# Moving the adaptive norm's sums to GpSimd beside mixer and queries and to VectorE beside the gated stage, with row sums behind their chunk's split

## Chip, cores and metric

One core of a Trainium2 chip runs the whole kernel. The metric is device time in microseconds of one execution. Engines carry the profile's names: PE (TensorE), DVE (VectorE), ACT (ScalarE), POOL (GpSimd) and SP (SyncE, which issues most loads).

## What is computed

Two blocks on 512 tokens of width 1024, in float32. The first block has a mixer (convolution and pooling), a feed-forward layer that picks 16 of 16384 experts for each of 8 heads and token, and a gated projection. The second has two attention layers, each with an adaptive norm whose shift, scale and gate come from a condition vector for the tokens and one for a context of 256 rows. Cut to what matters:

```python
h = h + concat([y_conv, y_pool]) @ w_o                     # mixer
# experts, on xn = rms_norm(h)
q = (xb @ w_q).reshape(T, 8, 2, 128)                       # queries
s = einsum('thpd,hpkd->thpk', q, sub_keys)                 # scores; top 16, pairs, top 16 again
act = gelu(einsum('thkd,td->thk', expert_u[eidx], xb))
h = h + einsum('thk,thkd->td', gate * act, expert_v[eidx])
# gated stage
h = h + sigmoid(rms_norm(h) @ w_ple_gate) * (p @ w_ple_proj)
# second block, for layer i in (0, 1); the same for the context rows with c_ctx
shift, scale, gate = split(silu(c) @ ada_w[i] + ada_b[i], 3)
hx = rms_norm(x, norm_g[i]) * (1 + scale) + shift
x = x + gate * attention_i(hx, hc)
```

`ada_w` is 2 x 1024 x 3072. The change concerns how `silu(c) @ ada_w` is summed, and when.

## The kernel before

The stages follow one another: mixer, queries, expert chunks, expert products, gated stage, attention A, attention B. Matrix products in float32 are made of two halves: ACT writes the rounded high half (`wh`, line 93), DVE subtracts it for the low one (`wl`, line 94), and three matmuls are summed (lines 104 to 106). Each engine works through its instructions in order; a planner sets that order when the program is built, from the order of the code, from due times and from `issue_after`, which puts an instruction behind another on its engine.

**Mixer** (`mix`). The 16 column blocks of `w_in` go through `proj`, then `w_o` by token blocks of 128. When a token block is complete, `norm.add` begins the next normalisation: ACT sums squares, POOL takes the row scale in two small instructions (`rstat`, lines 112 and 113, written `rn`), DVE scales (`xs`), and PE flips the result into `x`. POOL's other work here is two casts, eight fills and these row scales.

**Queries and chunks** (`peer`). Sixteen queries, each with one chunk of `expert_u` beside it; then the routing of four token blocks with the rest of the 128 chunks (`chunk`). Tokens 0 to 127 are done by rows that are gathered (class `Gathered`): for each of 128 choices a row per token of `expert_r` comes by a gather on POOL and DVE takes a dot product (line 442); later a row of `expert_v` comes and DVE adds it, weighted, into `h` (line 453, `sums`). Tokens 128 to 511 (384 columns) go through all 16384 experts: gate weights are written out to `Gd` and activations to `Hd`, both in DRAM. A pace factor of 1.2 sets how many gathers go beside one unit of routing.

**Products** (`peer_out`). For each of the 128 chunks a load brings `gt` (every fourth chunk) and `ht` (every second) from `Gd` and `Hd`, DVE multiplies them (`pr`, line 702), the product is split (`xn_0h`, `xn_0l` to `xn_7l`), `expert_v` is loaded and split (`wl`), and 18 matmuls follow (lines 715, 716, 718). Row sums are drawn at 1.1 a chunk. Here, too, the adaptive norm's sums lie: 48 loads of 512 KB (`araw`, on SP's queue), 88 scalings or multiply-adds on DVE (`aacc`, lines 777 and 780; one operand column per 128 rows of `ada_w`), then folds of partition halves through ACT copies and POOL additions (lines 796 to 802). One step is drawn for every pair of chunks.

**Gated stage** (`ple`) and after. Between its token blocks `finish` turns the sums into columns by small matmuls, adds the biases and keeps shift and scale in `ada_aff` and the gate in DRAM. Attention A begins with its weights (`a_qkv`) on the same SP queue, and its last step is `gate_residual`.

## Time and profile before

| | us |
|---|---|
| median of 3 runs (lowest, highest) | 2477.11 (2474.19, 2484.84) |
| the profiled execution, its own time | 2475.35 |
| its span, first to last instruction | 2473.6 |
| PE busy in it | 2264.6 |
| DVE busy in it | 1897.8 |
| POOL busy in it | 739.8 |

The span is what the trace shows; the execution's time has 1.8 us around it. Busy times are sums over a span in which several stages with different limits follow one another; a stage is read by its own stretch of the trace. The mean granted TensorE clock is 0.968 of full speed.

### The profile page before, as it was taken

How to read it: one execution, taken by the hardware profiler on the slowest of the kernel's cores; microseconds unless marked ns; L12 is line 12 of the kernel's file. 1: busy time of each engine (PE TensorE's matmuls, PEld its weight loads, DVE VectorE, ACT ScalarE, POOL GpSimd, SP SyncE). 2: the span in 40 equal slices, each digit the busy share in tenths (PEclk: the TensorE clock that was granted, in tenths of full speed). 3: DMA queues.
4: the chain of work that ended last, by engine and by line, in shares of the span. 5: the costliest groups of instructions: out<-in, count | busy, mean ns of one | idle time of the engine just before them, and what ended most of it. 6: DMA issues, size and time to landing. Idle time of an engine off the chain costs nothing. (4 is left out here: it accounts for less than half of the span.)

```text
span 2473.6 us, 34866 instructions
## 1 busy us (share of the span) xinstructions
PE 2264.6 (92%) x12611; PEld 1972.5 (80%) x12611; DVE 1897.8 (77%) x3431; ACT 1082.1 (44%) x1876; POOL 739.8 (30%) x745
## 2 busy tenths in 40 slices
PE   8999997999998939878888789989999999999997
PEld 6888887999998938766777567777888788898886
DVE  5567799999998879897988885473488955378884
ACT  4243333444443423332333333452477834466772
POOL 1000005334334452352443540031233323023331
PEclk9999998999999979999999899999999999999999
DMA  4233338999999899979989785332211032210002
GB/s 161 94 102 120 115 133 292 340 376 345 342 362 346 326 374 332 326 257 331 321 319 341 267 307 187 103 105 96 92 33 31 24 104 89 82 48 27 26 10 94
DMA packets 179084, 481.08 MB, mean 194 GB/s; under 512 B 15437, under 2 KB 68957, under 8 KB 177376
## 3 DMA queue, kind: packets, MB, share of 16 engines
q1 hardware_dynamic: 125840, 276.95, 32.9%
q0 software_dynamic: 42128, 151.57, 16.7%
q10 hardware_dynamic: 10944, 50.34, 5.0%
q8 instruction: 99, 1.62, 0.3%
q14 instruction: 73, 0.60, 0.1%
HBM read 419.02 MB, written 59.78 MB: 194 GB/s over the span
## 5 line engine op out<-in xcount | busy, mean ns | idle before, releaser
L93 ACT ACTIVATE wh<-raw 128x1024 fp32r<-128x1024 f32 (+2 forms) x371 | 388.6, 1050 | 705.1 <-DMA raw<-in_expert_v 180.8
L94 DVE TENSOR_TENSOR wl<-raw,wh 128x1024 fp32r<-128x1024 f32 (+2 forms) x371 | 453.4, 1226 | 124.2 <-ACT wh L93 119.8
L429 POOL DMA_INDIRECT grow<-in_expert_v,gidx x128 | 214.0, 1672 | 357.7 <-DVE h L453 312.1
L429 POOL DMA_INDIRECT grow<-in_expert_r,gidx x128 | 168.1, 1313 | 254.0 <-DVE gdot L442 229.9
L453 DVE SCALAR_TENSOR_TENSOR h<-grow,gdot,h 128x1024 f32<-128x1024 f32 x128 | 172.4, 1347 | 30.7 <-DMA grow<-in_expert_v,gidx 30.1
L442 DVE CUSTOM_DVE_ANT_0 gjunk<-grow,gx 128x1024 bf16<-128x1024 f32 x128 | 156.3, 1221 | 14.8 <-DMA grow<-in_expert_r,gidx 14.6
L929 DVE TENSOR_TENSOR ptl<-acc,pth 128x512 fp32r<-128x512 f32 x184 | 123.7, 687 | 30.5 <-ACT pth L928 29.0
L780 DVE SCALAR_TENSOR_TENSOR aacc<-araw,silu_c,aacc 128x1024 f32<-128x1024 f32 x77 | 97.7, 1282 | 54.1 <-DMA araw<-in_ada_w 53.9
L928 ACT ACTIVATE pth<-acc 128x512 fp32r<-128x512 f32 x184 | 106.3, 596 | 51.1 <-PE acc L1457 31.4
L1094 POOL TENSOR_SCALAR p<-p,st 128x256 f32<-128x256 f32 (+2 forms) x96 | 65.0, 678 | 135.8 <-DVE st L1093 96.3
L1438 POOL TENSOR_SCALAR p<-p,st 128x768 f32<-128x768 f32 x64 | 60.5, 946 | 127.0 <-DVE st L1437 104.1
L644 ACT ACTIVATE hs<-acc 128x384 f32<-128x384 f32 x128 | 61.1, 478 | 76.7 <-PE acc L106 76.5
L702 DVE TENSOR_TENSOR pr<-ht,gt 128x384 f32<-128x384 f32 x128 | 81.2, 653 | 2.3 <-DMA ht<-Hd 1.9
L106 PE MATMUL acc<-xn_0h,wl 128*128 128x384 f32 (+2 forms) x175 | 61.3, 350 | 23.5 <-DVE wl L94 23.5
L1092 ACT ACTIVATE p<-S,st 128x257 f32<-128x257 f32 (+2 forms) x96 | 62.9, 655 | 25.3 <-DVE st L1090 14.3
L524 POOL CAST sif<-si 128x256 bf16<-128x256 uint32 x4 | 6.5, 1633 | 200.8 <-DVE si L520 173.7
L613 PE MATMUL g<-oh,oh 128*128 128x128 f16 x768 | 54.6, 222 | 13.0 <-DVE oh L606 8.2
L104 PE MATMUL acc<-xn_0h,wh 128*128 128x384 f32 (+2 forms) x175 | 64.3, 367 | 1.3 <-ACT hs L644 1.1
L112 POOL TENSOR_SCALAR rn<-rn 128x1 f32<-128x1 f32 x34 | 10.8, 318 | 182.0 <-ACT xs L111 176.3
L1434 DVE TENSOR_REDUCE st<-S 128x1 f32<-128x768 f32 x64 | 60.8, 951 | 5.3 <-PE S L106 4.2
L1090 DVE TENSOR_REDUCE st<-S 128x1 f32<-128x257 f32 (+2 forms) x96 | 61.6, 643 | 3.5
L613 PEld LDWEIGHTS <-oh 128*128 128x128 f16 x768 | 46.0, 99 | 21.5 <-issue 12.6
(1144 smaller groups left out, 7606.9 us busy)
## 6 DMA issues: line engine op xcount, KB each, us to landing
raw<-in_expert_u SPq DMA_DIRECT2D x128, 512.0 KB
raw<-in_expert_v SPq DMA_DIRECT2D x128, 512.0 KB
Hd<-hs ACTq DMA_DIRECT2D x64, 384.0 KB
Gd<-gs ACTq DMA_DIRECT2D x12, 2048.0 KB
gt<-Gd SPq DMA_DIRECT2D x32, 768.0 KB
ht<-Hd SPq DMA_DIRECT2D x64, 384.0 KB
araw<-in_ada_w SPq DMA_DIRECT2D x48, 512.0 KB
raw<-in_w_in SPq DMA_DIRECT2D x16, 512.0 KB
```

Of the source, the lines that this page charges most:

```text
L93: nc.scalar.activation(hi[:, s], src[:, s], AF.Copy)
L94: (sub or nc.vector).tensor_tensor(lo[:, s], src[:, s], hi[:, s].bitcast(F32), OP.subtract)
L104: mm(out, a[0], b[0], start=start, stop=False)
L429: self.k.nc.gpsimd.indirect_dma_start(t, None, table, at)
L442: nc.vector.tensor_tensor_reduce(junk, t, self.x, 1.0, 0.0, OP.mult, OP.add, self.dot[:, s : s + 1])
L453: nc.vector.scalar_tensor_tensor(self.h, t, self.dot[:, s : s + 1], self.h, OP.mult, OP.add)
L613: nc.tensor.matmul(g[:, i], oh[2][at], oh[q][at], start=q == 0, stop=q == 1)
L702: nc.vector.tensor_tensor(by_g(pr), by_g(cur["h"][:, c % 2]), cur["g"][:, :, c % GC], OP.mult)
L780: nc.vector.scalar_tensor_tensor(a, raw, sc, a, OP.mult, OP.add)
L928: k.nc.scalar.activation(hi, src, AF.Copy)
L929: (eng or k.nc.vector).tensor_tensor(lo, src, hi.bitcast(F32), OP.subtract)
L1094: nc.gpsimd.tensor_scalar(p[:, :W], p[:, :W], st[:, 2:3], 1.0, OP.mult, OP.mult)
```

## The change

The sums of the adaptive norm leave `peer_out`. They are made on halves of 128x512 now. Layer 0 and the gate third of layer 1 are summed by POOL alone (a scaling and an addition for each term, loads on POOL's own queue), drawn two steps at a time in the mixer's projections, between token blocks of `w_o` and behind each query. Shift and scale of layer 1 are summed by DVE (multiply-adds of 128x512, loads on SP's queue) between token blocks of the gated stage and of the start of attention A. Sums go to DRAM; `finish(layer)` loads them back in halves of 64 rows, adds the halves on DVE and goes on by small matmuls, for layer 0 in the gated stage and for layer 1 in the last step of attention A. Besides, each row sum stands behind the low half of the newest split, the pace factor goes from 1.2 to 1.5, and in the mixer the buffer `c` is single and the product `yc` is made in place. The diff, cut to its core (the removed bodies of `work`, `fold` and `finish` are described above):

```diff
@@ split
-            (sub or nc.vector).tensor_tensor(lo[:, s], src[:, s], hi[:, s].bitcast(F32), OP.subtract)
+            self.wl = (sub or nc.vector).tensor_tensor(lo[:, s], src[:, s], hi[:, s].bitcast(F32), OP.subtract).ins
@@ rstat
-        nc.gpsimd.tensor_tensor(out, out, self.mhalf[:, :1], OP.pow)
+        self.rs = nc.gpsimd.tensor_tensor(out, out, self.mhalf[:, :1], OP.pow).ins
@@ mix
+        def some(n):
+            for _ in range(n):
+                next(work, None)
+
         def proj(nb):
             uh, ul = unit if nb == 12 else k.unit(ap["w_in"][nb])
+            some(2)
             return now(k.fm(x, 8, uh, ul, [0]))
...
-            c = mp.tile([P, T], F32, tag="c", name=k.nm("c"), bufs=2)
+            c = mp.tile([P, T], F32, tag="c", name=k.nm("c"), bufs=1)
...
-            yc = mp.tile([P, T], F32, tag="yc", name=k.nm("yc"), bufs=2)
-            nc.vector.tensor_tensor(yc, y, psb, OP.mult)
-            put_split(k, *yf.run(g, 0), yc)
+            nc.vector.tensor_tensor(y, y, psb, OP.mult)
+            put_split(k, *yf.run(g, 0), y)
...
-        k.tm(yf, 8, [tm_units(ap["w_o"], 4 * nh, 2, 4) for nh in range(2)], range(TB), evac)
+        units = [tm_units(ap["w_o"], 4 * nh, 2, 4) for nh in range(2)]
+        k.tm(yf, 8, units, range(TB), evac, between=8 * [lambda: some(2)])
@@ Gathered.sums
-            nc.vector.scalar_tensor_tensor(self.h, t, self.dot[:, s : s + 1], self.h, OP.mult, OP.add)
+            with self.k.tc.issue_after(self.k.wl):
+                nc.vector.scalar_tensor_tensor(self.h, t, self.dot[:, s : s + 1], self.h, OP.mult, OP.add)
@@ peer
-                    spent -= c * 1.2
+                    spent -= c * 1.5
...
         query(hp)
+        for _ in range(2):
+            next(work, None)
         chunk(c)
         c += 1
+    for _ in work:
+        pass
...
-    adp = adx.enter_context(tc.tile_pool(name="adp", bufs=1, side="right"))
-    ada = Ada(k, adp, hs[1])
@@ peer_out
-            if c < NCH - 2:
-                next(ada, None)
-        for _ in ada:
-            pass
@@ Ada
-    def work(self, pool):
+    def work(self, pool, thirds, gpsimd):
...
+        for layer, third, half in [(l, t, s) for l, t in thirds for s in range(2)]:
+            conds = self.conds(layer, third)
+            at = third * 1024 + half * 512
+            acc = [pool.tile([P, 512], F32, tag="aacc", name=k.nm("aacc"), bufs=2) for _ in conds]
+            for kc in range(8):
+                raw = pool.tile([P, 512], F32, tag="araw", name=k.nm("araw"), bufs=3)
+                w = k.ap["ada_w"][layer, kc, :, at : at + 512]
+                if gpsimd:
+                    with k.tc.issue_after(k.rs):
+                        nc.gpsimd.dma_start(raw, w)
+                else:
+                    nc.sync.dma_start(raw, w)
+                for cond, a in enumerate(acc):
+                    sc = self.s[:, cond * 8 + kc : cond * 8 + kc + 1]
+                    if kc == 0:
+                        (nc.gpsimd if gpsimd else nc.vector).tensor_scalar(a, raw, sc, 1.0, OP.mult, OP.mult)
+                    elif gpsimd:
+                        t = raw
+                        if cond + 1 < len(conds):
+                            t = pool.tile([P, 512], F32, tag="atmp", name=k.nm("atmp"), bufs=1)
+                        nc.gpsimd.tensor_scalar(t, raw, sc, 1.0, OP.mult, OP.mult)
+                        nc.gpsimd.tensor_tensor(a, a, t, OP.add)
+                    else:
+                        nc.vector.scalar_tensor_tensor(a, raw, sc, a, OP.mult, OP.add)
                 yield
-                if third == 1:
-                    self.fold(pool, self.acc[layer, 0, 0], pair[0], 32)
-                    yield
-        self.fold(pool, self.acc[0, 0, 2], pair[0], 32)
+            for cond, a in enumerate(acc):
+                nc.gpsimd.dma_start(self.parts[layer, third, half][cond], a)
+            yield
-    def finish(self):
+    def finish(self, layer):
...
+            def folded(third, half):
+                t = [fp.tile([P, 512], F32, tag="afold", name=k.nm("afold"), bufs=4) for _ in range(2)]
+                m = 64 * len(self.conds(layer, third))
+                for i in range(2):
+                    for c in range(m // 64):
+                        s = slice(64 * c, 64 * c + 64)
+                        nc.sync.dma_start(t[i][s], self.parts[layer, third, half][c, 64 * i : 64 * i + 64])
+                nc.vector.tensor_tensor(t[0][:m], t[0][:m], t[1][:m], OP.add)
+                return t[0][:m], sel[:m, third]
@@ ple
-            ada.finish()
-            adx.close()
+            ada.finish(0)
+            apool = adx.enter_context(tc.tile_pool(name="adq", bufs=1, side="right"))
+            rest.append(ada.work(apool, [(1, 0), (1, 1)], False))
...
+        def later():
+            for _ in range(2):
+                next(rest[0], None)
...
-        k.tm(x, 8, units, range(TB), evac, between=[before.pop(0), conditions, context])
+        k.tm(x, 8, units, range(TB), evac, between=[before.pop(0), conditions, context] + 5 * [later])
...
-    return [lambda: flip(0), lambda: flip(1), norm[0].close]
+    return [lambda: flip(0), lambda: flip(1), norm[0].close] + 13 * [later] + [end]
@@ gate_residual
+                    if tb == 5:
+                        ada.finish(1)
@@ the whole kernel
+        ada = Ada(k)
+        work = ada.work(adx.enter_context(tc.tile_pool(name="adp", bufs=1, side="right")), [(0, 0), (0, 1), (0, 2), (1, 2)], True)
         qw = Query(k)
-        before, xs = mix(k, h, x, qw.load)
-        ada, before, pT = peer(k, h, x, adx, qw, before, xs)
+        before, xs = mix(k, h, x, qw.load, work)
+        before, pT = peer(k, h, x, work, adx, qw, before, xs)
```

On POOL, around the row scale of the first token block that comes out of the mixer (`rn_1068` before, `rn_1338` after; `u` and `z` are the mixer's tiles, `araw` a load of `ada_w`, `atmp` a scaled term, `aacc` a sum). Before:

```order
L305 MEMSET u_710 128x8
L306 MEMSET u_710 128x8
L342 MEMSET z_827 128x1
L343 MEMSET z_827 128x1
L112 TENSOR_SCALAR rn_1068<-rn_1068 128x1
L113 TENSOR_TENSOR rn_1068<-rn_1068,mhalf 128x1
L112 TENSOR_SCALAR rn_1100<-rn_1100 128x1
L113 TENSOR_TENSOR rn_1100<-rn_1100,mhalf 128x1
```

After:

```order
L795 TENSOR_TENSOR aacc_1236<-aacc_1236,araw_1241 128x512
L795 TENSOR_TENSOR aacc_1235<-aacc_1235,atmp_1276 128x512
L794 TENSOR_SCALAR araw_1274<-araw_1274,silu_c 128x512
L794 TENSOR_SCALAR atmp_1283<-araw_1281,silu_c 128x512
L795 TENSOR_TENSOR aacc_1236<-aacc_1236,araw_1274 128x512
L795 TENSOR_TENSOR aacc_1235<-aacc_1235,atmp_1283 128x512
L794 TENSOR_SCALAR araw_1281<-araw_1281,silu_c 128x512
L795 TENSOR_TENSOR aacc_1236<-aacc_1236,araw_1281 128x512
L112 TENSOR_SCALAR rn_1338<-rn_1338 128x1
L113 TENSOR_TENSOR rn_1338<-rn_1338,mhalf 128x1
```

Before, the row scale follows the last fill. After it, 72 scalings, 62 additions and 44 issues of loads and stores of the adaptive norm stand between the first norm and it, and between it and the last of the four row scales another ten, eight and seven.

On DVE, in the middle of the products (`h_58` is the sum of token block 0, `pr` the product of gate and activation). Before:

```order
L777 TENSOR_SCALAR aacc_10437<-araw_10435,silu_c 128x1024
L94 TENSOR_TENSOR wl_10380<-raw_10377,wh_10379 128x1024
L777 TENSOR_SCALAR aacc_10439<-araw_10435,silu_c 128x1024
L929 TENSOR_TENSOR xn_2l_95<-pr_10516,xn_2h_94 128x384
L453 SCALAR_TENSOR_TENSOR h_58<-grow_11014,gdot,h_58 128x1024
L929 TENSOR_TENSOR xn_3l_97<-pr_10547,xn_3h_96 128x384
L94 TENSOR_TENSOR wl_10411<-raw_10408,wh_10410 128x1024
L702 TENSOR_TENSOR pr_10617<-ht_10584,gt_10582 128x384
L702 TENSOR_TENSOR pr_10654<-ht_10652,gt_10582 128x384
L453 SCALAR_TENSOR_TENSOR h_58<-grow_11045,gdot,h_58 128x1024
L780 SCALAR_TENSOR_TENSOR aacc_10437<-araw_10510,silu_c,aacc_10437 128x1024
```

After:

```order
L94 TENSOR_TENSOR wl_11039<-raw_11036,wh_11038 128x1024
L460 SCALAR_TENSOR_TENSOR h_58<-grow_11042,gdot,h_58 128x1024
L945 TENSOR_TENSOR xn_5l_101<-pr_11196,xn_5h_100 128x384
L712 TENSOR_TENSOR pr_11295<-ht_11293,gt_11291 128x384
L94 TENSOR_TENSOR wl_11070<-raw_11067,wh_11069 128x1024
L460 SCALAR_TENSOR_TENSOR h_58<-grow_11073,gdot,h_58 128x1024
L460 SCALAR_TENSOR_TENSOR h_58<-grow_11076,gdot,h_58 128x1024
L945 TENSOR_TENSOR xn_6l_103<-pr_11229,xn_6h_102 128x384
L94 TENSOR_TENSOR wl_11106<-raw_11103,wh_11105 128x1024
L460 SCALAR_TENSOR_TENSOR h_58<-grow_11109,gdot,h_58 128x1024
L712 TENSOR_TENSOR pr_11326<-ht_11293,gt_11291 128x384
```

The `aacc` rows are gone, and each `h_58` stands right behind a `wl`. Before, 36 of the 128 row sums stand ahead of the first `pr`; after, none.

On SP, the loads of the gated stage and the start of attention A. Before:

```order
L99 DMA raw_13958<-in_w_pg 128x1024
L99 DMA raw_13964<-in_w_pg 128x1024
L99 DMA raw_13970<-in_w_pg 128x1024
L99 DMA raw_14173<-in_a_qkv 128x1024
L99 DMA raw_14179<-in_a_qkv 128x1024
L99 DMA raw_14185<-in_a_qkv 128x1024
```

After:

```order
L785 DMA araw_14233<-in_ada_w 128x512
L785 DMA araw_14279<-in_ada_w 128x512
L785 DMA araw_14283<-in_ada_w 128x512
L785 DMA araw_14329<-in_ada_w 128x512
L785 DMA araw_14333<-in_ada_w 128x512
L785 DMA araw_14383<-in_ada_w 128x512
L785 DMA araw_14738<-in_ada_w 128x512
L99 DMA raw_14181<-in_w_pg 128x1024
L99 DMA raw_14416<-in_a_qkv 128x1024
L785 DMA araw_14742<-in_ada_w 128x512
L99 DMA raw_14422<-in_a_qkv 128x1024
```

The last load of the gate's weights, `raw_13970` before and `raw_14181` after, stands behind seven loads of `ada_w`.

## Rows read from the trace of the kernel before

**Rows 1.** The page, part 1: busy us (share), instructions of each engine.

```profile
PE 2264.6 (92%) x12611; PEld 1972.5 (80%) x12611; DVE 1897.8 (77%) x3431; ACT 1082.1 (44%) x1876; POOL 739.8 (30%) x745
```

**Rows 2.** Windows; busy us (count): PE, PEld, DVE, ACT, POOL; clock; DMA share; GB/s.

```profile
24.00:136.00 112.00, 112.00 (x493) 92.22 (x492) 62.83 (x91) 34.78 (x44) 1.26 (x9) 1.00 0.37 119
160.00:365.00 205.00, 202.37 (x1084) 183.09 (x1083) 168.79 (x678) 74.66 (x118) 5.70 (x4) 1.00 0.36 117
410.00:780.00 370.00, 363.22 (x2411) 356.99 (x2410) 358.44 (x605) 153.82 (x229) 141.69 (x108) 1.00 0.94 350
780.00:895.00 115.00, 100.48 (x713) 96.66 (x712) 103.61 (x132) 45.82 (x73) 53.82 (x34) 0.94 0.90 333
895.00:930.00 35.00, 1.49 (x4) 1.16 (x4) 20.41 (x19) 3.65 (x7) 17.99 (x14) 0.56 1.04 402
930.00:1500.00 570.00, 490.71 (x2004) 391.53 (x2003) 496.72 (x530) 195.95 (x253) 220.30 (x112) 0.93 0.87 309
1560.00:1680.00 120.00, 111.45 (x525) 85.22 (x524) 73.47 (x127) 65.47 (x115) 27.61 (x49) 1.00 0.28 91
```

**Rows 3.** Waits, 900 to 1510: line waited for; us in total, times, longest.

```profile
PE acc L716 <- DVE wl L94: 75.0, 30, 9.6
DVE aacc L780 <- DMA araw<-in_ada_w: 53.9, 24, 9.0
PE o L715 <- ACT xn_0h L928: 34.3, 1, 34.3
DVE h L453 <- DMA grow<-in_expert_v,gidx: 21.0, 11, 6.2
```

**Rows 4.** Timeline of POOL, row scales: start, duration, instruction, [idle before <- releaser].

```profile
11.32 0.55 POOL L113 TENSOR_TENSOR rn<-rn,mhalf 128x1 f32<-128x1 f32 x1
136.63 0.19 POOL L112 TENSOR_SCALAR rn<-rn 128x1 f32<-128x1 f32 x1 [76.63 <-ACT xs L111]
154.42 0.19 POOL L112 TENSOR_SCALAR rn<-rn 128x1 f32<-128x1 f32 x1 [2.40 <-ACT xs L111]
```

**Rows 5.** Groups on POOL, 1600 to 2473: instruction xcount | busy, mean ns | idle before.

```profile
L1094 POOL TENSOR_SCALAR p<-p,st 128x512 f32<-128x512 f32 x32 | 22.9, 718 | 41.3 <-DVE st L1093 36.8 <-PE acc L1070 2.0 <-PE acc L106 1.9
L953 POOL TENSOR_TENSOR qr<-qr,rope 128x512 f32<-128x512 f32 x8 | 10.3, 1283 | 32.3 <-DVE rope L950 32.3
L1005 POOL DMA_DIRECT2D Qd<-qr x12 | 6.7, 559 | 20.5 <-ACT qr L1004 18.2 <-POOL qr L953 2.4
```

**Rows 6.** Timeline of POOL and of DVE at a fold.

```profile
981.61 3.35 POOL L800 TENSOR_TENSOR aacc<-aacc,fold 64x1024 f32<-64x1024 f32 x1 [8.48 <-ACT fold L796]
982.62 2.76 DVE L929 TENSOR_TENSOR xn_0l<-pr,xn_0h 128x384 fp32r<-128x384 f32 x1
```

**Rows 7.** Groups on DVE, 928 to 1560.

```profile
L94 DVE TENSOR_TENSOR wl<-raw,wh 128x1024 fp32r<-128x1024 f32 x125 | 156.6, 1253 | 15.8 <-ACT wh L93 15.7
L453 DVE SCALAR_TENSOR_TENSOR h<-grow,gdot,h 128x1024 f32<-128x1024 f32 x92 | 126.2, 1372 | 7.1 <-DMA grow<-in_expert_v,gidx 6.9
L780 DVE SCALAR_TENSOR_TENSOR aacc<-araw,silu_c,aacc 128x1024 f32<-128x1024 f32 x77 | 97.7, 1282 | 54.1 <-DMA araw<-in_ada_w 53.9
L702 DVE TENSOR_TENSOR pr<-ht,gt 128x384 f32<-128x384 f32 x127 | 80.8, 654 | 2.3 <-DMA ht<-Hd 1.9
L929 DVE TENSOR_TENSOR xn_7l<-pr,xn_7h 128x384 fp32r<-128x384 f32 x16 | 8.8, 553 | 3.6 <-ACT xn_7h L928 3.6
```

**Rows 8.** Timeline of PE in the products: first, two chunk starts, last.

```profile
928.51 0.79 PE L715 MATMUL o<-wh,xn_0h 128*128 128x512 f32 x1 [34.28 <-ACT xn_0h L928]
...
1530.87 0.39 PE L715 MATMUL acc<-wh,xn_7h 128*128 128x512 f32 x1
...
1534.95 0.39 PE L715 MATMUL acc<-wh,xn_0h 128*128 128x512 f32 x1
...
1567.14 0.62 PE L718 MATMUL o<-wh,xn_7l 128*128 128x512 f32 x2
```

**Rows 9.** Timeline of SP's queue in the gap.

```profile
910.17 0.39 SPq L693 DMA_DIRECT2D gt<-Gd  x1
```

More of the change, by code (lines that the diff above doesn't have):

```diff
@@ L276, in tm_units, with mix @@
     return [(src[first + i], kcs) for i in range(count)]
-def mix(k, h, x, ahead):
+def mix(k, h, x, ahead, work):
     tc, nc, ap = k.tc, k.nc, k.ap
@@ L670, in peer, with peer_out @@
     norm = Norm(k, D, 4, 5)
-    xs, pT = peer_out(k, h, x, Gd, Hd, ada.work(op), op, norm, (hs[2], hs[1]), few)
+    xs, pT = peer_out(k, h, x, Gd, Hd, op, norm, (hs[2], hs[1]), few)
     second.close()
     hsx.close()
-    return ada, flips(k, norm, xs, x, "g_ple"), pT
-def peer_out(k, h, x, Gd, Hd, ada, pp, norm, after, few):
+    return flips(k, norm, xs, x, "g_ple"), pT
+def peer_out(k, h, x, Gd, Hd, pp, norm, after, few):
     tc, nc, ap = k.tc, k.nc, k.ap
@@ L758, in __init__, with conds @@
         self.gate = k.dp.tile([3, D], F32, name="gate_d")
[L760 removed]
+        self.parts = {
+            (l, t, s): k.dp.tile([2, P, 512], F32, name=f"ada{l}{t}{s}") for l in range(2) for t in range(3) for s in range(2)
+        }
+    @staticmethod
+    def conds(layer, third):
+        return (0, 1) if layer == 0 or third < 2 else (0,)
+    def work(self, pool, thirds, gpsimd):
         k = self.k
         nc = k.nc
[L763 to L788 removed]
@@ L790, in fold @@
-    def fold(self, pool, a, b, w, both=2):
-        nc = self.k.nc
-        t = pool.tile([P, 1024], F32, tag="araw", name=self.k.nm("fold"), bufs=2)
-        parts = [(slice(c, c + w), slice(c + w, c + 2 * w)) for c in range(0, P, 2 * w)]
-        for lower, upper in parts:
-            nc.scalar.activation(t[lower], a[upper], AF.Copy)
-            if both == 2:
-                nc.scalar.activation(t[upper], b[lower], AF.Copy)
-        for lower, upper in parts:
-            nc.gpsimd.tensor_tensor(a[lower], a[lower], t[lower], OP.add)
-            if both == 2:
-                nc.gpsimd.tensor_tensor(a[upper], b[upper], t[upper], OP.add)
@@ new lines, in finish @@
+            for third in range(3):
+                for cond in range(2):
+                    c = cond if third == 2 else 2 * cond + third
+                    nc.gpsimd.memset(sel[64 * cond : 64 * cond + 64, third, c : c + 1], 1.0)
+            bias = fp.tile([P, D], F32, name=k.nm("gb"))
+            for i in range(n):
+                nc.gpsimd.dma_start(bias[i : i + 1], k.ap["row"][:, 2048 + layer * 1024 : 3072 + layer * 1024])
+            def folded(third, half):
[7 more added lines that the diff above has]
+                return t[0][:m], sel[:m, third]
@@ L832, in finish @@
+            aff = fp.tile([P, D], F32, name=k.nm("affr"))
+            for half in range(2):
+                s = slice(half * 512, half * 512 + 512)
+                ps = k.acc()
+                for third in range(2):
+                    t, w = folded(third, half)
+                    nc.tensor.matmul(ps[:4], w, t, start=third == 0, stop=third == 1)
+                nc.scalar.activation(aff[0:4, s], ps[:4], AF.Copy)
             tr = k.acc()
             for b in range(8):
-                nc.tensor.transpose(tr[:, b * 8 : b * 8 + 8], aff[0:8, b * P : (b + 1) * P], k.ident[0:8, 0:8])
@@ L843, in finish @@
                 nc.vector.scalar_tensor_tensor(o[:, 8:16], o[:, 8:16], 1.0, k.colt[:, g0:g1], OP.add, OP.mult)
-            rows(
-                [(2, self.acc[0, 0, 2])],
-                3,
-                lambda s, ps: nc.vector.tensor_tensor(bias[0:3, s], ps, bias[0:3, s], OP.add),
-            )
-            nc.gpsimd.dma_start(self.gate, bias[0:3])
+            for half in range(2):
+                s = slice(half * 512, half * 512 + 512)
+                ps = k.acc()
+                t, w = folded(2, half)
+                nc.tensor.matmul(ps[:n], w[:, :n], t, start=True, stop=True)
+                nc.vector.tensor_tensor(bias[0:n, s], ps[:n], bias[0:n, s], OP.add)
+            nc.gpsimd.dma_start(self.gate[2 * layer : 2 * layer + n], bias[0:n])
 def affine_of(k, ada, feat, cond, run):
@@ L889, in context @@
             norm[0].flip([norm[0].add(f) for f in loads], affine_of(k, ada, xc, 1, 0))
-        norm = []
+        norm, rest = [], []
         xs = []
```

66 lines of the change are left out of this document (15 added, 51 removed).

## The prediction

> **What bounds the kernel now.** The page's first part was read first: TensorE (PE) is busy 92% of the span, VectorE (DVE) 77%, GpSimd (POOL) 30% [rows 1]. A mean over stages with different limits says little, so the table by stage came next [rows 2]. The reader is to see four things in it. In the mixer (24 to 136 us) and the queries (160 to 365) PE is the bound, busy for 112.00 of 112 and 202.37 of 205 us, with DVE at 62.83 and 168.79 and POOL almost idle. In the first routing stretch (410 to 780) PE and DVE are both near full, with 350 GB/s of DMA. From 895 to 930 PE does nothing. In the expert products (930 to 1500) PE is busy 490.71 of 570 us at a clock of 0.93, and DVE 496.72. The stage table thus names the places where time can be won: the gap and the products. The wait table of 900 to 1510 us says for whom PE waits there [rows 3]: 75.0 us in 30 waits for the low halves that DVE splits off (`wl`), and once 34.3 us for the first product's operand. DVE itself waits 53.9 us in 24 waits for `araw`, the loads of the adaptive norm. One chunk late in the stage takes 1534.95 - 1530.87 = 4.08 us, so 128 chunks need 522 us; the stage runs from 928.51 to 1567.8, 639 us, which is 117 us over that floor [rows 8].
>
> **The change, part by part.** The profiled execution took 2475.35 us, of which the span is 2473.6; the median of the three runs is 1.8 above it. The sum is made against 2475.35, and 1.8 added at the end.
>
> *Products, a gain of 90 us.* The 88 multiply-adds of the adaptive norm leave DVE here: 77 at 1282 ns [rows 7] are 99 us, and eleven that only start a sum come on top. Against them 36 row sums come in, since all 128 stand behind a split now instead of 92: 36 x 1372 ns [rows 7] = 49 us. DVE's work per chunk then is one `pr` of 0.55 to 0.65, one low half `xn` of 0.55 to 0.69, one `wl` of 1.25 and 1.1 row sums of 1.37, together 3.9 to 4.1 us [rows 7], beside PE's 4.08. The 57 us of waits for `araw` go with the loads, and so do the folds on POOL, which block DVE (below). DMA per chunk stays: 0.52 MB of `expert_v`, 0.39 of the two DRAM tables, 1.1 x 0.52 gathered, 1.49 MB; at 4.25 us that is 350 GB/s, the rate which the stretch 410 to 780 carried with PE at 98% [rows 2]. What is late next is DVE itself, in order and without slack. I take 4.25 us a chunk, 544 us, and 5 us of ends: 639 - 549 = 90. Bounds: 112 with PE at its floor and the same ends, 57 if only the waits for `araw` go and all else is paid back.
>
> *The gap, a gain of 12.* The first `gt` load is issued at 910.17 [rows 9], when the last 2 MB store of the gate table has landed; in the gap DMA moves 402 GB/s at a share of 1.04 [rows 2], and the rows gathered for the sums are among it, which no longer run there. I take a third of the 35 us away; 5 to 18 are the bounds, since the store, the load and the multiplication keep their order.
>
> *Chunks beside routing, a gain of 10.* 36 row sums of 1.37 us leave a stretch (780 to 895) in which DVE is busy 103.61 of 115 us and PE 100.48 [rows 2], 49 us of DVE in all. PE's idle time there is 14.5 us, and the pace factor of 1.5 feeds fewer gathers per unit of routing. I take 10, bounds 0 and 20.
>
> *Mixer to queries, a loss of 71.* This is the largest cost. Ahead of the next norm's first row scale on POOL (`rn_1338`) now stand 44 DMA issues, 72 scalings and 62 additions of 128x512, in program order. A scaling of that shape takes 0.718 us, an addition 1.283, a DMA issue 0.559 [rows 5]: 51.7 + 79.5 + 24.6 = 156 us. They start when the first norm is through on POOL, at 11.87 [rows 4], and a load has come, some 3 us: row scale not before 171 us, against 136.63 [rows 4]. Ten more scalings, eight additions, seven issues and three row scales lie between the first and the last of the four row scales: 24 us. The last thus comes at 195 at the earliest, where it stood at 154.42 [rows 4]: 41 us of loss with POOL undisturbed. It isn't. In the fold at 981.61 POOL's addition takes 3.35 us and ends at 984.96; DVE's subtraction begun at 982.62 takes 2.76 us instead of 0.55 and ends at 985.38, 0.42 us after it [rows 6, 7]: POOL shuts DVE out. DVE works 62.83 us in the mixer [rows 2], most of it on two operands in SBUF. If all of it stops POOL, the row scale comes at 234, a loss of 104. I take 30 us of it, about half, because no row shows a DMA issue (a sixth of POOL's time) or a DVE read from PSUM colliding: 201, the last one at 225, a loss of 71. The scaled rows are what the flips for the queries need, DVE's and PE's own queues stand behind them, and PE has nothing else: of this nothing is covered.
>
> The Trainium skill, "SBUF — State Buffer", section "Who interferes with whom", makes the collision a rule: a DVE instruction with two SBUF inputs and a GpSimd one that reads SBUF share a port pair under an exclusive lock, and the later one is blocked for the whole instruction. The rows at 981.61 agree. Taken to the letter for all of DVE's time, the rule gives the 104 and a sum 33 us worse; without it, 41 and 30 us better. The same rule speaks for the products, where POOL's folds go.
>
> *Queries, a loss of 5.* 30 more scalings, 28 additions and 27 issues, 73 us by the same rows, lie on POOL beside 168.79 us of DVE and 205 us of stage [rows 2]. PE stays the bound as long as blocking adds under 36 us to DVE; bounds 0 and 20.
>
> *Gated stage, a loss of 12.* 64 sums of 128x512 on DVE, at half of the 1282 ns of the 128x1024 form [rows 7], are 41 us. In 1560 to 1680 DVE is busy 73.47 of 120 us and PE 111.45 [rows 2], so they fit by time and not by order: seven `araw` loads stand ahead of the last gate weight on SP's queue, each waiting for a buffer that DVE frees. Nothing is lost if the idle time takes all; 25 if each sum pushes back a busy DVE as often as it meets one (61%). I take the middle.
>
> *The two finishes, a loss of 7.* Partial sums go through DRAM, and each finish waits for loads before a few small additions and matmuls. The nearest row is DVE's wait for `araw`, 53.9 us in 24, 2.2 each [rows 3]; three such lie on the path, bounds 0 and 15. The in-place product and the single `c` buffer cost nothing: PE's blocks of four projections lie between two uses.
>
> Losses 71 + 5 + 12 + 7 = 95, gains 90 + 12 + 10 = 112: 17 us less, 2458, and with 1.8 **2460 us**.
>
> **Rivals.** *POOL runs beside DVE undisturbed*: the row scale comes at 171, the loss is 41 and the queries lose nothing: 35 us better, 2425. For it: DMA issues and PSUM reads fill much of the stretch; against it: both rows of the collision. *The row sums keep PE waiting* (the slower side): each sum sits behind a split and waits for a gather, and the next split sits behind it. If gathers are late, as 11 times for 21.0 us now [rows 3], the chunk goes above 4.4 us, the products give 57 and the routing stage nothing: 43 us worse, 2503. For it: 1.1 gathers a chunk instead of 0.7, and DVE with no slack; against: DMA carried the same rate from 410 to 780. It turns the sign from a chunk of about 4.4 us on. *POOL is shut out by all of DVE's work*: loss 104, queries 20, so 48 us worse, 2508. For it: a train of DVE operations can keep POOL out to its end; against: half the mixer's POOL time falls where DVE idles. That the change doesn't do what it says is no case here: both orders show the sums where they are said to be.
>
> **How the numbers follow.** Forecast 0.45, with a range of its own from 2440 to 2485; undisturbed POOL 0.20; late row sums 0.18; shut-out 0.17. A measurement of this kernel can tell about 0.5% (12.4 us) from no change: faster means below 2464.7, slower above 2489.5. Forecast: faster 0.24, same 0.18, slower 0.03. Undisturbed: faster 0.20. Late sums: slower 0.15, same 0.03. Shut-out: slower 0.11, same 0.06. Together faster 0.44, same 0.27, slower 0.29. The range goes from 2418 to 2510, which takes in all four times and the nearer half of their bounds.
>
> **What would show it.** The first row scale of the second norm on POOL near 200 us and PE idle for some 70 us around 150 to 230 would bear out the largest loss; 170 the first rival; 230 the last. DVE subtractions longer than 2 us in the mixer show the collision. In the products, chunks of 4.25 us, no wait for `araw`, and fewer than 30 us of PE waiting for `wl` bear out the gain; row sums waiting for gathers, with PE behind, the second rival. A PE gap of some 20 us before the products shows the third term. The forecast is wrong if the sums on POOL end before the mixer does, or if the products stay above 570 us.

## The result, and the profile after

The changed kernel takes 2448.39 us, the median of four runs (2443.73 to 2457.12), beside 2475.65 of the kernel before (four runs here, where the table above has three); the ratio of the two is 0.9883 with a 95% interval of 0.9853 to 0.9912. It is 1.2% faster. The profiled execution took 2457.12, the slowest of the four, beside 2475.35 before: what the traces can account for is 18 us, not the 27 between the medians.

Where these 18 us come from is read off five landmarks of the two traces. The rows are instruction groups (count, shortest, median and longest duration in ns, first and last start in us): the gate matmuls of the routing, the high-half matmuls of the products' first operand, the gated stage's first step, the stores of the rotated queries in attention A, and the stores of its result. Before:

```profile
L613 PE MATMUL g<-oh,oh x768: 217/218/312, 448.4 to 894.0; 128*128 128x128 f16 x192
L715 PE MATMUL o<-wh,xn_0h x48: 387/389/794, 928.5 to 1538.1; 128*128 128x512 f32 x48
L897 ACT ACTIVATE sg<-acc x8: 579/598/600, 1587.3 to 1638.7; 128x512 f32<-128x512 f32 x8
L1005 POOL DMA_DIRECT2D Qd<-qr x12: 542/559/599, 1696.2 to 1760.1; - x12
L1215 POOL DMA_DIRECT2D x2d<-x x8: 547/576/615, 2026.0 to 2063.6; - x8
```

After:

```profile
L620 PE MATMUL g<-oh,oh x768: 217/218/330, 532.2 to 957.4; 128*128 128x128 f16 x192
L725 PE MATMUL o<-wh,xn_0h x48: 389/389/397, 986.7 to 1483.4; 128*128 128x512 f32 x48
L904 ACT ACTIVATE sg<-acc x8: 578/597/601, 1532.6 to 1595.5; 128x512 f32<-128x512 f32 x8
L1021 POOL DMA_DIRECT2D Qd<-qr x12: 539/557/557, 1654.9 to 1718.8; - x12
L1231 POOL DMA_DIRECT2D x2d<-x x8: 544/569/630, 1990.5 to 2046.5; - x8
```

Beside them stand the row scales that come out of the mixer, on POOL's timeline (before: 136.63 and 154.42, [rows 4]):

```profile
204.83 0.19 POOL L112 TENSOR_SCALAR rn<-rn 128x1 f32<-128x1 f32 x1
237.51 0.19 POOL L112 TENSOR_SCALAR rn<-rn 128x1 f32<-128x1 f32 x1
```

| stretch | before | after | change | predicted |
|---|---|---|---|---|
| last row scale behind the mixer | 154.4 | 237.5 | +83.1 | +71 |
| from there to the first gate matmul | 294.0 | 294.7 | +0.7 | +5 |
| first gate matmul to first product | 480.1 | 454.5 | -25.6 | -22 |
| first product to first step of the gated stage | 658.8 | 545.9 | -112.9 | -90 |
| from there to the last store of queries (with the finish of layer 0) | 172.8 | 186.2 | +13.4 | +12, and a part of 7 |
| from there to the last store of attention A (with the finish of layer 1) | 303.5 | 327.7 | +24.2 | the rest of 7 |
| the rest of the span | 410.0 | 408.8 | -1.2 | 0 |
| sum | | | -18.3 | -17 |

The page's busy line: PE works as long as before (2264.6 us [rows 1]), POOL 163 us longer.

```profile
PE 2271.6 (93%) x12631; PEld 1979.8 (81%) x12631; DVE 1858.9 (76%) x3421; ACT 1061.2 (43%) x1855; POOL 902.5 (37%) x1021
```

The table by stage (length; busy us and instructions of PE, PEld, DVE, ACT, POOL; granted clock; DMA share; GB/s) answers to [rows 2]:

```profile
24.00:136.00 112.00, 95.96 (x387) 75.65 (x388) 98.25 (x84) 29.62 (x39) 106.76 (x104) 0.92 0.46 153
160.00:365.00 205.00, 146.39 (x745) 127.96 (x744) 109.28 (x405) 54.86 (x93) 151.78 (x170) 0.84 0.41 134
957.00:990.00 33.00, 33.00 (x195) 32.41 (x193) 18.71 (x21) 13.71 (x22) 6.74 (x4) 1.00 0.92 319
990.00:1480.00 490.00, 488.44 (x2147) 403.42 (x2146) 417.49 (x491) 186.43 (x245) 140.19 (x122) 1.00 0.99 358
1532.00:1600.00 68.00, 58.60 (x237) 40.55 (x236) 53.15 (x89) 28.24 (x49) 20.22 (x29) 0.90 0.55 174
1972.00:2047.00 75.00, 66.24 (x260) 47.31 (x259) 35.83 (x62) 18.37 (x29) 21.75 (x44) 0.86 0.49 148
```

In the mixer (first row) POOL is full, 106.76 of 112 us, DVE has gone from 62.83 to 98.25 us with fewer instructions, and PE from 112.00 to 95.96. In the stretch that was the queries PE is busy 146.39 of 205 us, at a mean granted clock of 0.84 (1.00 before [rows 2]). The gap of 35 us ahead of the products is gone (third row: 33.00 of 33), and in the products (fourth) PE is busy 488.44 of 490 us at full clock, with 358 GB/s of DMA. The last two rows hold the two finishes, with a mean granted clock of 0.90 and 0.86; the like stretches before, 1587 to 1639 and 2012 to 2064, have 1.00.

The wait table of 160 to 240 us, and that of 1000 to 1480 behind the dots (us in total, times, longest), say the same of PE: 41.1 us for scaled rows, and in the products, where it had waited 75.0 us for low halves [rows 3], 0.8.

```profile
PE tr L228 <- DVE xs L217: 41.1, 2, 29.6
...
PE acc L726 <- DVE wl L94: 0.8, 1, 0.8
```

### The profile page after: what moved, and what is told of

Its sections match the earlier page's. It is cut to its first block, busy times and chain, and to the rows that moved or that the text cites. A ratio compares the mean times of both kernels' runs of the same rounds, so it can differ in the third digit from the quotient of the medians.

```text
span 2455.3 us, 35344 instructions
## 1 busy us (share of the span) xinstructions
PE 2271.6 (93%) x12631; PEld 1979.8 (81%) x12631; DVE 1858.9 (76%) x3421; ACT 1061.2 (43%) x1855; POOL 902.5 (37%) x1021
## 5 line engine op out<-in xcount | busy, mean ns | idle before, releaser
L94 DVE TENSOR_TENSOR wl<-raw,wh 128x1024 fp32r<-128x1024 f32 (+2 forms) x371 | 465.4, 1259 | 138.3 <-ACT wh L93 133.0
L435 POOL DMA_INDIRECT grow<-in_expert_v,gidx x128 | 151.8, 1186 | 347.7 <-DVE h L460 329.8
L460 DVE SCALAR_TENSOR_TENSOR h<-grow,gdot,h 128x1024 f32<-128x1024 f32 x128 | 163.7, 1279 | 0.4
L228 PE MATMUL tr<-ident,xs 128*128 128x128 f32 x220 | 46.3, 339 | 69.3 <-DVE xs L217 56.3
L228 PEld LDWEIGHTS tr<-ident,xs 128*128 128x128 f32 x220 | 32.4, 172 | 83.2 <-issue 31.2
L712 DVE TENSOR_TENSOR pr<-ht,gt 128x384 f32<-128x384 f32 x128 | 70.9, 557 | 15.5 <-DMA ht<-Hd 12.0
L795 POOL TENSOR_TENSOR aacc<-aacc,araw 128x512 f32<-128x512 f32 x56 | 77.0, 1374 | 1.3
L217 DVE TENSOR_SCALAR xs<-h,rn 128x1024 f32<-128x1024 f32 x16 | 12.5, 783 | 79.2 <-POOL rn L113 78.9
L613 DVE TENSOR_TENSOR oh<-oh,gb 128x1024 f16<-128x1024 f16 x96 | 61.8, 683 | 7.5 <-PE g L620 7.5
```

The lines of the kernel that those rows point to most:

```text
L94: self.wl = (sub or nc.vector).tensor_tensor(lo[:, s], src[:, s], hi[:, s].bitcast(F32), OP.subtract).ins
L228: k.nc.tensor.transpose(ps[:, i * P : (i + 1) * P], x[:, kc * P : (kc + 1) * P], k.ident)
L435: self.k.nc.gpsimd.indirect_dma_start(t, None, table, at)
L460: nc.vector.scalar_tensor_tensor(self.h, t, self.dot[:, s : s + 1], self.h, OP.mult, OP.add)
L795: nc.gpsimd.tensor_tensor(a, a, t, OP.add)
```

## The experiments

Ratios are to runs of the kernel before on the same chip; the changed kernel's own is 0.9883. "The stage of the products" is always counted from the first product to the first step of the gated stage, 658.8 us before and 545.9 after.

**The mixer: the first term only.**

```diff
-            for kc in range(8):
+            for kc in range(1 if gpsimd else 8):
```

> The changed kernel with only the first of the eight terms of each half that GpSimd sums; the other seven terms (loads, scalings, additions) are left out. Theory (GpSimd's sums ahead of the row scales are what holds the restart behind the mixer): the first row scale comes at 137 to 142 us instead of 204.8, the last at about 156, PE has no gap there, and the time falls by 75 to 85 us from 2448 to 2363 to 2373. Rival (the restart is late for another reason, such as the loads of the adaptive norm or the single c buffer): the row scale stays beyond 180 and the time falls by less than 30, to 2418 or more.

Measured: 2358.16 us, ratio 0.9503 (0.9476 to 0.9530), so by the ratios some 94 us below the changed kernel. The mixer's stretch, and the row scales on POOL:

```profile
24.00:136.00 112.00, 112.00 (x493) 92.18 (x492) 64.88 (x90) 35.15 (x45) 22.15 (x38) 1.00 0.45 155
...
L112 POOL TENSOR_SCALAR rn<-rn x4: 182/188/190, 136.1 to 153.9; 128x1 f32<-128x1 f32 x4
```

PE is busy 112.00 of 112 us again and the row scales run from 136.1 to 153.9, as before the change. GpSimd's sums are what holds the restart; the gain is 9 us over the upper end expected.

**The mixer: row scales off GpSimd's queue.** The run above takes queue and collisions away together. This one leaves every sum where it is and takes the four row scales to other engines:

```diff
-        nc.gpsimd.tensor_scalar(out, out, 1.0 / width, EPS, OP.mult, OP.add)
-        self.rs = nc.gpsimd.tensor_tensor(out, out, self.mhalf[:, :1], OP.pow).ins
+        eng.tensor_scalar(out, out, 1.0 / width, EPS, OP.mult, OP.add)
+        if eng is nc.gpsimd:
+            self.rs = nc.gpsimd.tensor_tensor(out, out, self.mhalf[:, :1], OP.pow).ins
+        else:
+            nc.scalar.activation(out, out, AF.Sqrt)
+            eng.reciprocal(out, out)
...
-                xs.append(norm.add(h[tb]))
+                xs.append(norm.add(h[tb], nc.vector))
```

> The changed kernel, in which the four row scales behind the mixer are taken by a multiply-add and a reciprocal on VectorE around a square root on ScalarE, so that they don't stand in GpSimd's queue; all sums stay where they are. Theory (the queue on GpSimd is the price, the collisions with VectorE only the smaller part): the last row scale comes at 165 to 180, the sums end on GpSimd at about 320 beside the queries, the time falls by 55 to 70 to 2378 to 2393. Rival (the collisions on the shared side are the price): the mixer and the queries stretch as long as GpSimd sums, PE has stalls of 40 us or more in 24 to 350, and the time falls by 0 to 25, to 2423 to 2448.

Measured: 2389.77 us, ratio 0.9643 (0.9606 to 0.9680), 60 us below the changed kernel and the fastest whole version of this study. The mixer's stretch, the last step of the row scales, now on DVE, and the gate matmuls:

```profile
24.00:136.00 112.00, 96.87 (x402) 78.18 (x403) 98.06 (x86) 30.05 (x39) 107.57 (x106) 0.92 0.47 158
...
L118 DVE RECIPROCAL rn<-rn x4: 154/164/164, 160.4 to 177.8; 128x1 f32<-128x1 f32 x4
...
L625 PE MATMUL g<-oh,oh x768: 217/218/330, 473.2 to 895.8; 128*128 128x128 f16 x192
```

The first row reads like that of the changed kernel (POOL 107.57, DVE 98.06, PE 96.87): the collisions are all there. The row scales end at 177.8 instead of 237.5, and the first gate matmul comes at 473.2 instead of 532.2. Of the 83.8 us by which the changed kernel is late there (448.4 before), the queue on POOL thus costs 59 and the stretched mixer 25. In the run with early loads below, whose instructions are the same up to there, the first gate matmul comes at 484.9, which makes it 47 and 37; the parts are known no better than that.

**The products: the order of the row sums alone,** in the kernel before:

```diff
-            nc.vector.scalar_tensor_tensor(self.h, t, self.dot[:, s : s + 1], self.h, OP.mult, OP.add)
+            with self.k.tc.issue_after(self.k.wl):
+                nc.vector.scalar_tensor_tensor(self.h, t, self.dot[:, s : s + 1], self.h, OP.mult, OP.add)
```

> The kernel before with one part of the change alone: each row sum stands behind the newest chunk's split; the adaptive norm's sums stay in the products. Theory (the products gain because the adaptive norm's work leaves them, not by the order): 36 row sums move from the routing stage into products that are already short of VectorE, so these take 639 us or up to 40 more, routing and gap give back 5 to 25, and the time stays within 20 us of before. Rival (the order of row sums and splits is what made PE wait): the products fall to 600 us or less and the time by 25 us or more.

Measured: 2471.21 us, ratio 0.9953 (0.9936 to 0.9971). The same groups as among the landmarks:

```profile
L614 PE MATMUL g<-oh,oh x768: 217/218/308, 451.6 to 888.6; 128*128 128x128 f16 x192
L716 PE MATMUL o<-wh,xn_0h x48: 387/389/796, 910.0 to 1536.7; 128*128 128x512 f32 x48
L898 ACT ACTIVATE sg<-acc x8: 579/597/600, 1586.0 to 1637.3; 128x512 f32<-128x512 f32 x8
```

The stage of the products takes 1586.0 - 910.0 = 676.0 us, 17 more than before; from the first gate matmul to the first product it is 458.4 instead of 480.1. As expected, and the sign is worth noting: alone, the order lengthens the products, by row sums that left the stretch ahead of them; both stretches together take 1134.4 us instead of 1138.9.

**The products: everything but that order,** the changed kernel without it:

```diff
-            with self.k.tc.issue_after(self.k.wl):
-                nc.vector.scalar_tensor_tensor(self.h, t, self.dot[:, s : s + 1], self.h, OP.mult, OP.add)
+            nc.vector.scalar_tensor_tensor(self.h, t, self.dot[:, s : s + 1], self.h, OP.mult, OP.add)
```

> The changed kernel without its order of row sums (they stand where the planner puts them, as before). Theory: the products stay at 520 to 545 us, the gap ahead of them comes back in part because gathers run in it again, and the time is 0 to 20 us above the changed kernel's 2448 to 2453. Rival (the order is needed): the products take 560 us or more, the time 2480 or more.

Measured: 2497.37 us, ratio 1.0061 (1.0043 to 1.0078): slower than the kernel before. Here the theory fell, and the rival holds. The stage of the products takes 1573.1 - 990.7 = 582.4 us, 36 more than with the order, so the adaptive norm's leaving is worth only 76 of the 113 by itself. Two stretches of 60 us, waits of 1000 to 1310, and the row sums:

```profile
1120.00:1180.00 60.00, 56.18 (x232) 45.06 (x231) 52.94 (x61) 19.16 (x26) 33.84 (x22) 0.94 1.04 391
1360.00:1420.00 60.00, 60.00 (x266) 49.69 (x265) 32.59 (x45) 23.46 (x30) 0.00 (x0) 1.00 0.70 229
...
ACT wh L93 <- DMA raw<-in_expert_v: 178.2, 54, 9.8
POOL grow L435 <- DVE h L459: 136.1, 92, 10.9
...
L459 DVE SCALAR_TENSOR_TENSOR h<-grow,gdot,h x128: 1269/1277/1330, 943.9 to 1311.8; 128x1024 f32<-128x1024 f32 x128
```

The same of the changed kernel:

```profile
1120.00:1180.00 60.00, 60.00 (x266) 49.67 (x266) 52.50 (x63) 22.44 (x31) 17.44 (x17) 1.00 1.05 386
...
ACT wh L93 <- DMA raw<-in_expert_v: 87.7, 40, 5.9
POOL grow L435 <- DVE h L460: 214.1, 76, 9.6
...
L460 DVE SCALAR_TENSOR_TENSOR h<-grow,gdot,h x128: 1276/1278/1285, 978.4 to 1450.1; 128x1024 f32<-128x1024 f32 x128
```

Without the order the row sums are through at 1311.8; with it they last until 1450.1. While they run ahead, DMA moves 391 GB/s at a share of 1.04, ACT waits 178.2 us for the chunks' own loads, and PE does 232 matmuls in 60 us. When they are over, PE does 266, its full rate. With the order the same share of 1.05 and 386 GB/s go by, but in step with the chunks: ACT waits 87.7 us for their loads, and PE does 266 throughout. The order is a brake on the gathers. A gather needs a buffer (`grow`) that a row sum sets free, and with the order POOL waits 214.1 us for row sums where it waits 136.1 without; in the 60 us from 1120 it issues 17 gathers instead of 22.

**The products: the folds, and the sums.** Two parts of the adaptive norm's work, each left out of the kernel before: the folds (copies on ACT, additions on POOL), then six of each eight multiply-adds on DVE.

```diff
-                self.fold(pool, pair[0], pair[-1], 64, len(conds))
...
-                    self.fold(pool, self.acc[layer, 0, 0], pair[0], 32)
...
-        self.fold(pool, self.acc[0, 0, 2], pair[0], 32)
```

> The kernel before with the folds left out (the copies on ScalarE and the additions on GpSimd that join partition halves of the adaptive norm's sums); its loads and VectorE's multiply-adds stay. Theory (the folds block VectorE for longer than they last): the stretches with folds hold 157, 177, 193 and 212 matmuls in 60 us where the others hold about 235, which is 45 us; the products fall from 639 to 585 to 605 us. Rival (the folds fill time that is lost anyway): 620 to 640.

Measured: 2428.97 us, ratio 0.9789 (0.9756 to 0.9823).

```profile
L715 PE MATMUL o<-wh,xn_0h x48: 389/389/795, 929.0 to 1490.0; 128*128 128x512 f32 x48
L894 ACT ACTIVATE sg<-acc x8: 578/598/600, 1539.2 to 1591.1; 128x512 f32<-128x512 f32 x8
```

The stage takes 1539.2 - 929.0 = 610.2 us, 49 less, as expected. A row sum there takes 1277 ns on average instead of 1373, a `pr` 550 instead of 647 (both from 930 to 1480): the folds had stretched DVE's own work. By the ratios, leaving out the folds alone takes more off the time than the whole change does; a change that moves only them was not tried.

```diff
-                        else:
+                        elif kc == 7:
                             a = self.acc[layer, cond, third]
                             nc.vector.scalar_tensor_tensor(a, raw, sc, a, OP.mult, OP.add)
```

> The kernel before with six of each eight multiply-adds of the adaptive norm on VectorE left out; its loads and folds stay. Theory: 66 x 1.28 = 84 us of VectorE and most of the waits for araw go, the products fall by 45 to 80 us to 560 to 595. Rival (VectorE's sums fit beside PE, the folds and the DMA are the price): the products fall by less than 25, to 615 or more.

Measured: 2457.03 us, ratio 0.9903 (0.9872 to 0.9933).

```profile
L715 PE MATMUL o<-wh,xn_0h x48: 389/389/796, 930.3 to 1517.9; 128*128 128x512 f32 x48
L897 ACT ACTIVATE sg<-acc x8: 577/598/600, 1567.1 to 1618.5; 128x512 f32<-128x512 f32 x8
L453 DVE SCALAR_TENSOR_TENSOR h<-grow,gdot,h x128: 1268/1277/3512, 821.6 to 1281.6; 128x1024 f32<-128x1024 f32 x128
```

1567.1 - 930.3 = 636.8 us, 22 less where 45 to 80 were expected. But the row sums are through at 1281.6 here, against 1468.5 before: what DVE was freed from, it spent on row sums, and their gathers ran ahead as in the run without the order. So this run doesn't show what DVE's sums cost; it shows that taking most of them away alone gives 22 us, within the bound of the rival.

**The pace factor,** back to 1.2 in the changed kernel:

```diff
-                    spent -= c * 1.5
+                    spent -= c * 1.2
```

> The changed kernel with the pace factor of 1.2 as before. Theory (the factor matters little: what it leaves for the gap it takes from routing): from the first gate matmul to the first product 450 to 465 us as now (454.5), a gap without PE of 10 to 25 us, the time within 10 us of the changed kernel's 2448 to 2453. Rival (the factor of 1.5 is what closes the gap): that stretch takes 470 to 490 us, the time 2465 to 2490.

Measured: 2458.61 us, ratio 0.9915 (0.9891 to 0.9939), not told apart from the changed kernel. PE's wait for the first product is back:

```profile
PE o L725 <- ACT xn_0h L944: 20.7, 1, 20.7
```

From the first gate matmul to the first product it takes 996.1 - 539.8 = 456.3 us, beside 454.5 with the factor of 1.5. The theory holds: the factor moves chunks into the gap; it makes nothing shorter.

**The finish of layer 1, moved ahead** to the end of attention A's projections:

```diff
+        ada.finish(1)
         sgp = es.enter_context(tc.tile_pool(name="asg", bufs=1, side="right"))
...
-                    if tb == 5:
-                        ada.finish(1)
```

> The changed kernel with the finish of layer 1 moved ahead: from between the token blocks of attention A's last step to the end of attention A's projections. Theory (the last step loses its 23 us because VectorE stands in line for the partial sums' loads): the last step's first to last load of x1 takes 30 to 35 us instead of 56, a part of the wait appears at the new place, and the time falls by 13 to 23, to 2425 to 2435. Rival (the finish costs the same wherever it stands): the time stays at 2443 to 2453.

Measured: 2457.45 us, ratio 0.9902 (0.9872 to 0.9932).

```profile
L1021 POOL DMA_DIRECT2D Qd<-qr x12: 539/557/559, 1646.1 to 1710.0; - x12
L1280 POOL DMA_DIRECT2D res<-x1d x8: 536/537/630, 1996.1 to 2026.1; - x8
L1232 POOL DMA_DIRECT2D x2d<-x x8: 544/580/619, 2008.1 to 2045.7; - x8
```

The last step's loads of `x1` now span 30.0 us instead of 56.0, but from the last store of queries to the last store of attention A it takes 335.7 us instead of 327.7: what the last step gained, the new place lost with 8 us on top. The rival holds. Together with the row scales on DVE:

> Row scales behind the mixer on VectorE and ScalarE, and the finish of layer 1 moved ahead, together. Theory: the two gains add up, 2358 to 2378. Rival: no more than the better of the two alone.

Measured: 2416.21 us, ratio 0.9726 (0.9673 to 0.9780), 26 us worse than the row scales alone. Half of that is the finish: from the last store of queries to that of attention A it takes 335.7 us again, where the row scales alone have 322.4. The other 14 are there at the first gate matmul (487.0 instead of 473.2), a stretch that the finish doesn't touch.

**The finish of layer 1, with early loads,** on top of the row scales on DVE:

```diff
+            got = ada.fetch(1, yp)      # loads eight of the twelve tiles ahead of the last step
...
-                        ada.finish(1)
+                        ada.finish(1, got)
```

> The row scales behind the mixer on VectorE and ScalarE (2390 us so far), and in addition eight of the twelve tiles of layer 1's partial sums are loaded at the start of attention A's last step, so that its finish finds them; the finish keeps its place. Theory (the 23 us of the last step are VectorE and PE standing in line for these loads): the last step's first to last load of x1 falls from 52 to 38 to 44 us, the time to 2374 to 2383. Rival (the small matmuls in float32 and the slower clock behind them are the price): no change, 2386 to 2394.

Measured: 2396.04 us, ratio 0.9653 (0.9624 to 0.9681), not told apart from 0.9643: the time of the theory was missed. The last step of the row scales, and the loads of `x1`:

```profile
L118 DVE RECIPROCAL rn<-rn x4: 149/156/164, 163.7 to 188.2; 128x1 f32<-128x1 f32 x4
...
L1299 POOL DMA_DIRECT2D res<-x1d x8: 536/547/628, 1923.4 to 1967.7; - x8
```

The `x1` loads span 44.3 us instead of 51.7, and the stretch to the last store of attention A is 5 us shorter (317.6 instead of 322.4), while the mixer, whose order of instructions is the same in both kernels, ended 10 us later (188.2 instead of 177.8). A gain of 5 us can't be seen in the times behind that.

**More sums on GpSimd,** on top of the early loads:

```diff
-[(0, 0), (0, 1), (0, 2), (1, 2)], True)
+[(0, 0), (0, 1), (0, 2), (1, 2), (1, 0)], True)
...
-[(1, 0), (1, 1)], False)
+[(1, 1)], False)
```

> As the run with the early loads, and the shift of layer 1 is summed by GpSimd, too (three steps behind each query instead of two), which leaves VectorE 32 sums beside the gated stage instead of 64. Theory (each sum on VectorE costs 0.1 to 0.2 us there, GpSimd is free until routing begins): 5 to 10 us less than that run, 2365 to 2377. Rival (GpSimd's sums then reach into the routing and hold up its gathers): 10 us more or worse, 2385 to 2400.

Measured: 2428.79 us, ratio 0.9788 (0.9755 to 0.9820): the rival, and by more than it said.

```profile
365.00:480.00 115.00, 69.92 (x361) 67.79 (x360) 76.55 (x209) 24.58 (x34) 58.26 (x60) 0.79 0.48 167
...
L625 PE MATMUL g<-oh,oh x768: 217/218/330, 516.5 to 939.5; 128*128 128x128 f16 x192
```

The first gate matmul comes 32 us later (516.5 instead of 484.9), and in 365 to 480 PE is busy 69.92 of 115 us. POOL's sums last until 405.7 there, in the run with the early loads until 320.3; by the profile DVE waits once, for 32.2 us, for their last store, and the first gather of the routing comes at 446.4 instead of 413.8.

**The gated stage: layer 1's first terms only,** in the changed kernel:

```diff
-            for kc in range(8):
+            for kc in range(8 if gpsimd else 1):
```

> The changed kernel with only the first of the eight terms of each half that VectorE sums beside the gated stage; the other seven terms, their loads too, are left out. Theory (these sums and loads cost the gated stage its 14 us): the stretch from the first product's end to the first store of the rotated queries takes 10 to 14 us less, the time 2435 to 2443. Rival (the finish of layer 0 in line is the price): 0 to 5 us less.

Measured: 2444.90 us, ratio 0.9866 (0.9840 to 0.9892), not told apart from the changed kernel.

```profile
L904 ACT ACTIVATE sg<-acc x8: 579/598/601, 1522.5 to 1583.9; 128x512 f32<-128x512 f32 x8
L1021 POOL DMA_DIRECT2D Qd<-qr x12: 539/557/584, 1640.9 to 1704.9; - x12
```

From the gated stage's first step to the last store of queries it takes 182.4 us instead of 186.2. So 4 of that stretch's 13 us are 56 of the 64 sums with their loads: the rival. The other 9 are what is left over; the finish of layer 0, the other thing that the change has put there, was not taken out by itself.

## Why the prediction was right, and where its terms were off

Its sum was 17 us less; the traces show 18 less, the medians 27, so that 2448.39 lies 12 under the 2460 it gave. The sign holds, and so do the two large terms that decide it, in kind. That the sum is met within 1 us is luck: the mixer took 12 us more than written and the gated stage with the finishes 19 more, against 23 more from the products and 4 each from the gap and the queries.

- **Mixer to queries, 71; measured 83.** The steps hold: the row scale came at 204.83 where 201 was written, so POOL's own work and 30 us on top were the right sum. The half of DVE's time was a choice between two bounds; the two reasons given for it hold, since an issue of a load on POOL takes 585 ns there instead of 559, and DVE's `h<-h,acc`, which reads PSUM, 686 where it took 687. Both collide as the row at 981.61 had said [rows 6]: in the changed kernel a `wl` of the mixer takes 1778 ns instead of 1224, and an addition on POOL 1396 to 1453 instead of 1283 [rows 5].

```profile
L795 POOL TENSOR_TENSOR aacc<-aacc,atmp 128x512 f32<-128x512 f32 x35 | 50.9, 1453 | 0.8
L795 POOL TENSOR_TENSOR aacc<-aacc,araw 128x512 f32<-128x512 f32 x35 | 48.8, 1396 | 0.5
L794 POOL TENSOR_SCALAR araw<-araw,silu_c 128x512 f32<-128x512 f32 x35 | 36.4, 1040 | 0.1
L94 DVE TENSOR_TENSOR wl<-raw,wh 128x1024 fp32r<-128x1024 f32 x24 | 42.4, 1778 | 3.4 <-ACT wh L93 3.4
```

  What was short is the stretch from the first to the last row scale, 24 written and 33 taken. POOL waits 5.5 us for loads of `ada_w` there, which were priced at nothing, and only two of its operations are stretched (2.11 and 1.66 us). The run with row scales elsewhere parts the term: 47 to 59 us of queue, 25 to 37 of the stretched mixer. The first rival (POOL undisturbed) and the last (all of DVE's work) are both out.
- **The rule on the shared port pair** (the Trainium skill, "SBUF — State Buffer", "Who interferes with whom"), taken for all of DVE's time, gave 234 for the first row scale; 204.83 was measured. In kind the trace agrees with it, but not all of DVE's time stops POOL. POOL's scaling by one column, with one operand in SBUF, slowed down as well: 1040 ns instead of 718.
- **Queries, 5; measured 0.7.** No loss can be seen. In the run with the first terms only, the stretch is 442.1 - 153.9 = 288.2 us, so the sums may cost some 6 us that another part of the change gives back; this wasn't tested.
- **Gap and routing, 22; measured 25.6.** The sum held, the reason less so. Some 20 us of the gap were to stay; none did. It is closed by chunks that the pace factor leaves for it; with 1.2 it is back at 20.7 us and the whole stretch takes the same time. What shortened the stretch is that most of the 36 row sums left it: 458.4 us already in the kernel before with the order alone.
- **Products, 90; measured 113, a shade over the upper bound of 112.** Two steps failed. One is DVE's price, 3.9 to 4.1 us a chunk and so "without slack": it was added up from rows that were taken beside the folds. In 990 to 1480 DVE is busy 417.49 us for some 119 chunks (2147 matmuls, 18 each), 3.5 us a chunk; a row sum takes 1279 ns instead of 1372 [rows 7], and as little in the kernel before without the folds. So PE stayed the bound, with 4.1 us a chunk instead of 4.25. The changed kernel from 990 to 1480, and behind the dots the run without folds from 930 to 1480:

```profile
L460 DVE SCALAR_TENSOR_TENSOR h<-grow,gdot,h 128x1024 f32<-128x1024 f32 x124 | 158.6, 1279 | 0.4
...
L453 DVE SCALAR_TENSOR_TENSOR h<-grow,gdot,h 128x1024 f32<-128x1024 f32 x92 | 117.5, 1277 | 0.4
```

  The other step is the order of the row sums, which was counted only as a cost of 49 us. The runs show 49 us for the folds alone and 22 for most of the sums alone, 71 together, about the 76 of the whole without the order; the order loses 17 there when it comes alone and gives 36 with the rest. It costs where DVE is short, and gives where DVE isn't, by keeping gathers in step with chunks. The second rival had it the other way round: it feared that each split would wait behind a gathered row. DVE had the room for it, 417.49 of 490 us.
- **Gated stage, 12, and both finishes, 7; measured 13 and 24, in all 38 instead of 19.** The term of the finishes is the one that was mis-sized: up to 9 for layer 0, by what is left over, and 24 for layer 1, against 4 for most of the 64 sums. (The six kernels that leave the finish of layer 1 as it is take 322.4 to 327.7 us for that stretch, so 24 is the upper end of 19 to 24.) It was priced at three waits of 2.2 us for loads, and left out PE's float32 matmuls and transposes, the order in which DVE and ACT pass them on, and the slower clock behind them. Moving it and loading ahead gave back little; which of these weighs most stays open.

## What to carry to other kernels

When work goes to an engine that has time, look for the two tiny instructions that this engine owes to everybody else: here four row scales behind sums that were priced at 156 us cost 47 to 59 us, and taking them to other engines gave 60 back and the fastest version of all. A brake on prefetching can decide the sign: without it the same change was slower than the kernel before. So test an order with and without the change that it came with; here it lost the products 17 us alone and gave them 36 with the rest. And price an engine's work from rows in which nothing collides with it, if the change takes the collisions away.

## What the runs showed of the hardware

With PE at 266 matmuls in 60 us, DMA moved 386 GB/s at a share of 1.05; at 391 GB/s without the order, it did 232, and chunk loads were late. So the rate didn't tell the two apart, but what was moved did: in 1120 to 1180, 17 gathers and 15 loads of `expert_v` were issued with the order, 22 and 12 without. The same instructions in the same order ended the mixer at 177.8 us in one kernel and at 188.0 to 188.3 in three others, all with sums on POOL beside DVE's work; with one trace of each it isn't shown whether the kernel or the execution makes these 10 us. With the row scales on POOL, behind all the sums, the last one comes at 236.0 to 238.0 in five kernels. A DVE operation that reads PSUM kept its time beside a busy POOL (686 ns, 687 before), a subtraction of two operands in SBUF did not (1778 instead of 1224).
